# First mixer: products for the block inverse right behind the keys, and a planner that counts PSUM banks

## The chip, the cores and the metric

The kernel runs on one core of one Trainium2 chip. The metric is the device time of one execution in microseconds (us). The engines are named as the profile names them: PE is TensorE (matmuls; PEld its weight loads), DVE is VectorE, ACT is ScalarE, POOL is GpSimd, SP is SyncE, which here only issues DMA transfers. Each engine works through its own list of instructions in order; they wait for each other on semaphores.

## The reference

The reference is a decoder trunk of two layers on 1024 tokens of width 1024, each layer a mixer and a SwiGLU feed-forward, with a final norm. The change lies in the mixer of layer 0, where two groups of eight heads share one input projection and one output projection:

```python
z = h @ w_in
z_ret, z_rwkv = z[..., :4 * RET_WIDTH], z[..., 4 * RET_WIDTH:]
...
o = chunk_retention(q, k, heads(v))
ret_out = head_group_norm(o, RET_GN_EPS).reshape(B, T, RET_WIDTH) * jax.nn.silu(g)
...
y = rwkv7_scan(r_h, heads(decay), k_h, v_h, -kk, kk * heads(a))
y = head_group_norm(y, RWKV_GN_EPS, ln_g, ln_b)
bonus = jnp.sum(r_h * k_h * r_k, axis=-1, keepdims=True) * v_h
rwkv_out = (y + bonus).reshape(B, T, RWKV_WIDTH) * gate

return jnp.concatenate([ret_out, rwkv_out], axis=-1) @ w_out
```

The scan updates a 64x64 state per head at every token with a decay and a rank-one delta rule. The kernel computes it in chunks of 64 tokens: within a chunk the delta rule is a triangular system, whose matrix is the masked product of the scaled keys with each other, and this has to be inverted.

## The kernel before, in words

The 1024 tokens are worked on in two halves of 512 (`hf` 0 and 1). The hidden state is stored transposed, eight tiles of 128 channels by 512 tokens. The input projection of a half is 30 jobs, and a job is one tile `ps_f` of 128 columns by 512 tokens: eight contraction steps with three matmuls each (weights and inputs are split into a high and a low part), 24 matmuls. Both halves together make the 1440 matmuls `ps_f<-n,w` of line 218. The weights of half 0 are split once and parked in DRAM (`wsp`), and half 1 loads them back.

Behind the projection stand two kinds of chains, written as Python generators that yield between their steps:
- `pair` (once for each pair of RWKV heads, four in a half): the low-rank products `wua`, the norm of the keys (line 606), the scaled tiles AR and BK (lines 630 to 640), the bonus sum `bv` (lines 651 to 653), then GG, the products BK x AR of both halves of the chunk, masked by DVE (line 668), their diagonal 32x32 blocks copied to DRAM (`dn`, line 674), and transposes of BK, AR and v (XA and UV).
- `unit` (once for two pairs; units 0 and 1 are of half 0, units 2 and 3 of half 1): the blocks come back from `dn` with one matrix per partition (DT, line 747), DVE inverts them in 62 small operations X (lines 758, 762), they go out to `dg` and back into the tiles GT (lines 766, 773), and transposes and two rounds of small products, TZ,GG and GT,TZ (`ps_c`), fill in the off-diagonal block. Then follow the products of XA, UV and GG with GT, the recurrence over the eight chunks (lines 852 to 859), y, its norm (lines 875 to 888) and the gate (lines 893 to 896), which is stored to `cat`.
- `ret` (once for each pair of retention heads) is a shorter chain of the same kind, from line 940 to 1024.
- `second_norm` squares and sums the inputs of half 1, takes their mean with one matmul over all channels (line 509 feeds it), loads the inputs again (line 521) and writes the normed high and low parts (lines 433, 434).

The order of the work is set when the program is built, by the class `Plan`. It keeps a made-up clock, `now`. It first offers a step to any generator whose needs have been met (named events with a delay behind each) and whose own yield delay has passed; if none is due, it emits three matmuls of the current projection job. The delays are numbers in the code, in us. What is emitted is the order on every engine, and on SP's queue; at run time the engines wait for each other wherever the plan was wrong. PSUM's eight banks are four for the small products (`ps_m`), three for `ps_f` and one for `ps_c`, each kind used in turn: the fifth `ps_m` waits until the first has been read.

When the projection jobs are through, the output projection of half 0 (lines 319 to 321, 24 matmuls for each of eight tiles) fills PE beside the last unit, and that of half 1 follows. From the output projection of half 1 on, the rest of the program (feed-forward, attention layer, second feed-forward) is emitted in an order of its own.

Of the kernel before, what the change touches and what calls it, by code (L numbers as in the profile page):

```python
# [104 lines left out]
class Plan:  # L105
# [3 lines left out]
    def __init__(self, K):  # L109
        self.K, self.now, self.ev = K, 0.0, {}  # L110
        self.gens, self.jobs, self.cur, self.ahead = [], deque(), None, 0
# [53 lines left out]
    def run(self):  # L165
        while self.gens or self.jobs or self.cur:
            nxt = []
            for g in self.gens:
                t = self.time(g[1], g[2])
                if t is not None and t <= self.now:  # L170
# [6 lines left out]
                if t is not None:  # L177
                    nxt.append(t)
# [8 lines left out]
class Kern:  # L187
    def __init__(self, ctx, tc, A, out):
# [12 lines left out]
        self.h = [None, None]  # L201
# [67 lines left out]
    def pst(self, tag, shape):  # L269
        return self.t(self.ps, shape, "ps_" + tag, self.psb[tag])  # L270
# [227 lines left out]
    def second_norm(self):  # L498
        nc = self.nc
        yield (("y0", 0.0),), 0.0  # L500
        acc = self.t(self.pp, [P, HT], "nq", 4)
        for k in range(KT):
# [7 lines left out]
            yield (), 3.0  # L510
        ps = self.pst("m", [P, HT])
# [39 lines left out]
    def shifted(self, hf, ti, nm, p):  # L551
# [25 lines left out]
        self.plan.job(f"{nm}{hf}_{p}", hf, 16 + ti, lambda: self.nT, evac, ((f"n{hf}", 0.0),))  # L577
# [5 lines left out]
    def pair(self, u, hf, p):  # L583
# [31 lines left out]
        yield (), 6.0  # L615
# [25 lines left out]
        yield ((f"r{hf}_{p}", 5.0), (f"v{hf}_{p}", 5.0)), 8.0  # L641
# [4 lines left out]
        yield (), 12.0  # L646
        if u:
            yield ((f"y{u - 1}", 1.0),), 0.0
# [5 lines left out]
        S.copy(vp[:, 0:64], vp[:, HT : HT + 64])  # L654

# [14 lines left out]
        dn = self.dns[u]  # L670
        for e in range(2):
            for b in range(2):
                q, r0 = (p % 2) * 4 + e * 2 + b, 64 * e + 32 * b
                nc.sync.dma_start(
                    dn[q * 8 : q * 8 + 8].rearrange("c s t -> s c t"), GG[r0 : r0 + 32, :, e, 32 * b : 32 * b + 32]
                )
        self.plan.done(f"n{u}_{p}")
# [47 lines left out]
        yield (), 5.0  # L725
# [9 lines left out]
    def unit(self, u, hf, pairs):  # L735
# [7 lines left out]
        yield tuple((f"n{u}_{p}", 3.5) for p in pairs), 0.0  # L743
# [4 lines left out]
        X = self.t(mp, [P, 16, 32], "X", 2)  # L748
# [6 lines left out]
        for j in range(31):  # L755
# [7 lines left out]
            if j % 2:  # L763
                yield (), 2.4
        for q in range(2):
            nc.sync.dma_start(dg.rearrange("u (i q) t -> q u i t", q=2)[q], X[64 * q : 64 * q + 64])
        GTs = [self.t(mp, [P, NCH, 64], "GT", 2) for _ in pairs]
# [8 lines left out]
        yield tuple((f"a{u}_{p}", 1.0) for p in pairs), 7.0  # L776
# [3 lines left out]
        for GT in GTs:  # L780
            TZ = self.t(mp, [P, 2, NCH, 32], "X", 2)
# [920 lines left out]
```

## Time and profile before

| | us |
|---|---|
| median of 3 runs | 2527.07 (2525.83 to 2533.37) |
| the profiled execution | 2525.36 |
| its span, first to last instruction | 2523.6 |
| PE busy | 2352.1 (93%) |
| DVE, ACT, POOL busy | 1629.1, 1037.1, 1315.3 |
| first mixer, from the start to the norm behind it | 0 to 788 |
| PE busy in the first mixer | 704.6 |

The profiled execution is 1.7 us under the median, and 1.8 us of it lie outside the span. A number of the profile counts each f32 matmul as two instructions, so a group that the program writes as 16 matmuls of 64x64 stands there as x32; the projection's matmuls, whose inputs are split already, count once. The granted clock (PEclk) is the share of full speed at which PE was let run: in a stretch of 0.5 a matmul takes twice its time.

### The profile page before, as it was taken

The numbers are of one execution on the slowest core, as the hardware profiler recorded it, in microseconds if no ns is written. First come the engines' busy times: TensorE is split into PE (matmuls) and PEld (weight loads), VectorE is DVE, ScalarE is ACT, GpSimd is POOL, SyncE is SP. The second block draws the span as 40 slices with busy tenths as digits, with TensorE's granted clock in tenths as the row PEclk, the third lists the DMA queues.
The fourth block names the chain that finished last, engine by engine and source line by source line (L and its number), as shares of the span: only waits on it lengthen the run. The fifth ranks groups of instructions, "written<-read, shape, count | busy, mean of one in ns | idle before, by whom it ended". The sixth has DMA issues, their size and how long they took to land.

```text
span 2523.6 us, 35280 instructions
## 1 busy us (share of the span) xinstructions
PE 2352.1 (93%) x12850; PEld 1833.2 (73%) x12850; DVE 1629.1 (65%) x2387; ACT 1037.1 (41%) x1907; POOL 1315.3 (52%) x1048
## 2 busy tenths in 40 slices
PE   8888798999888999999999999899998999998996
PEld 6666565776666778887778776677686788886785
DVE  3666855756446337878685448547627788777776
ACT  5344433233454433333333545446635233333335
POOL 6554331221446656776576433242247577767664
PEclk9999998999999999999999999999999999999998
DMA  7564552533344545564474222131235456646652
GB/s 279 184 202 145 162 182 86 152 133 104 122 161 152 200 150 179 200 217 155 151 270 167 94 76 68 42 131 68 98 133 172 144 200 216 218 176 220 247 205 86
DMA packets 169035, 400.61 MB, mean 159 GB/s; under 512 B 43040, under 2 KB 45728, under 8 KB 168864
## 3 DMA queue, kind: packets, MB, share of 16 engines
q1 hardware_dynamic: 165744, 392.87, 45.0%
q10 hardware_dynamic: 2832, 4.45, 0.5%
q8 instruction: 102, 1.67, 0.3%
q0 software_dynamic: 288, 1.05, 0.1%
q14 instruction: 69, 0.57, 0.1%
HBM read 272.34 MB, written 120.59 MB: 156 GB/s over the span
## 4 chain that ended last, share of the span: by engine, by line
PE 69%; DVE 14%; DMA 5%; ACT 5%; issue 3%; POOL 3%; SPq 1%; DVEq 0%; ACTq 0%; POOLq 0%
PE ps_f L218 6%; PE ps_m L1085 6%; PE ps_m L1086 6%; PE ps_m L1087 6%; PE ps_f L319 5%; PE ps_m L218 5%; PE ps_f L320 5%; PE ps_f L321 5%; PE ps_f L1086 3%; PE ps_f L1085 3%; PE ps_f L1087 3%; PE ps_r L1085 2%; PE ps_r L1086 2%; PE ps_r L1087 2%; PE ps_c L1085 2%
## 5 line engine op out<-in xcount | busy, mean ns | idle before, releaser
L305 POOL TENSOR_TENSOR w<-wr,w 128x512 fp32r<-128x512 f32 (+1 forms) x276 | 369.7, 1346 | 495.5 <-ACT w L304 456.1
L218 PE MATMUL ps_f<-n,w 128*128 128x512 f32 x1440 | 378.9, 412 | 5.2 <-DMA w<-wsp 3.9
L218 PEld LDWEIGHTS ps_f<-n,w 128*128 128x128 f32 x1440 | 268.6, 192 | 82.4 <-issue 19.6
L304 ACT CAST w<-wr 128x512 fp32r<-128x512 f32 (+1 forms) x276 | 166.6, 611 | 260.5 <-PE ps_f L321 147.9
L319 PE MATMUL ps_f<-n,w 128*128 128x512 f32 x496 | 199.9, 407 | 8.8 <-ACT n L325 4.3
L320 PE MATMUL ps_f<-n,w 128*128 128x512 f32 x496 | 198.7, 401 | 0.0
L1085 PE MATMUL ps_f<-n,w 128*128 128x512 f32 x453 | 181.5, 403 | 17.9 <-ACT u L1234 13.0
L321 PE MATMUL ps_f<-n,w 128*128 128x512 f32 x496 | 197.1, 399 | 0.3 <-POOL w L305 0.3
L1086 PE MATMUL ps_f<-n,w 128*128 128x512 f32 x453 | 179.7, 397 | 9.0 <-DVE n L327 6.3
L1087 PE MATMUL ps_f<-n,w 128*128 128x512 f32 x453 | 179.8, 398 | 5.9 <-POOL w L305 5.9
L305 POOL TENSOR_TENSOR w<-wq,w 128x512 fp32r<-128x512 f32 x86 | 124.1, 1455 | 37.2 <-ACT w L304 20.8
L1092 DVE TENSOR_TENSOR nq<-ps_m,u 128x512 f32<-128x512 f32 x88 | 58.7, 684 | 113.3 <-PE ps_m L1087 113.3
L327 POOL TENSOR_TENSOR n<-nq,n 128x512 fp32r<-128x512 f32 x69 | 115.3, 1683 | 16.5 <-ACT n L325 16.5
L1085 PEld LDWEIGHTS ps_f<-n,w 128*128 128x128 f32 x453 | 86.0, 190 | 46.6 <-ACT u L1234 18.4
L319 PEld LDWEIGHTS ps_f<-n,w 128*128 128x128 f32 x496 | 95.1, 192 | 33.9 <-ACT n L325 4.7
L320 PEld LDWEIGHTS ps_f<-n,w 128*128 128x128 f32 x496 | 95.0, 192 | 24.4 <-issue 4.7
L321 PEld LDWEIGHTS ps_f<-n,w 128*128 128x128 f32 x496 | 94.6, 191 | 23.0 <-issue 1.9
L1086 PEld LDWEIGHTS ps_f<-n,w 128*128 128x128 f32 x453 | 86.2, 190 | 29.2 <-DVE n L327 6.7
L1087 PEld LDWEIGHTS ps_f<-n,w 128*128 128x128 f32 x453 | 86.1, 190 | 26.9 <-POOL w L305 7.6
L1085 PE MATMUL ps_m<-cb,w 128*128 128x512 f32 x232 | 93.3, 402 | 9.5 <-DVE nq L1092 9.5
L1246 POOL TENSOR_TENSOR w<-wd,w 128x512 fp32r<-128x512 f32 (+1 forms) x53 | 75.4, 1429 | 47.3 <-ACT w L1245 43.5
L1087 PE MATMUL ps_m<-cb,w 128*128 128x512 f32 x232 | 93.1, 401 | 0.0
(503 smaller groups left out, 6136.3 us busy)
## 6 DMA issues: line engine op xcount, KB each, us to landing
hc<-n SPq DMA_DIRECT2D x74, 512.0 KB, 2.6
wsp<-w SPq DMA_DIRECT2D x60, 512.0 KB, 3.2
w<-wsp SPq DMA_DIRECT2D x60, 512.0 KB, 3.4
wq<-in_w_gate SPq DMA_DIRECT2D x44, 512.0 KB, 4.4
u<-u SPq DMA_DIRECT2D x88, 256.0 KB, 2.8
n<-hc SPq DMA_DIRECT2D x43, 512.0 KB, 5.7
hid<-n SPq DMA_DIRECT2D x66, 256.0 KB, 2.0
ha<-hc SPq DMA_DIRECT2D x33, 512.0 KB, 6.6
```

The lines of the kernel that those rows point to most:

```text
L218: i = self.nc.tensor.matmul(out, lhsT, rhs, **kw)
L304: nc.scalar.copy(hi[:, :n], raw[:, c])
L305: nc.gpsimd.tensor_tensor(out=lo[:, :n], in0=raw[:, c], in1=hi.bitcast(F32)[:, :n], op=ALU.subtract)
L319: nc.tensor.matmul(ps, hi, rh, start=k == 0, stop=False)
L320: nc.tensor.matmul(ps, hi, rl, start=False, stop=False)
L321: nc.tensor.matmul(ps, lo, rh, start=False, stop=k == n - 1)
L327: e.tensor_tensor(out=lo, in0=src, in1=hi.bitcast(F32), op=ALU.subtract)
L1085: mm(ps, hi, xh, start=first and k == 0, stop=False, skip_group_check=True)
L1086: mm(ps, hi, xl, start=False, stop=False, skip_group_check=True)
L1087: mm(ps, lo, xh, start=False, stop=last and k == len(w) - 1, skip_group_check=True)
L1092: add = lambda o, x, y: V.tensor_tensor(out=o, in0=x, in1=y, op=ALU.add)
L1246: nc.gpsimd.tensor_tensor(out=lo, in0=v, in1=hi.bitcast(F32), op=ALU.subtract)
```

## The change

It has five parts.

1. **Products of their own for the blocks** (`nd`). Right behind BK, each pair computes its key-by-key products into one PSUM tile (16 matmuls of 64x64), DVE masks them (line 665 after the change), and the diagonal blocks go to `dn` from there, in four transfers. Before, they were cut out of GG, which comes after r and v have been projected, after `bv`, and in a later unit after the unit before it has ended (`y` of that unit). GG is computed as before; the tile `nd` comes from the pool `rt`, of six buffers.
2. **Banks counted.** Each step that takes a `ps_m` tile notes it as taken for 3 us of the made-up clock. A generator is stepped only while fewer than three are taken, unless no projection work is ready.
3. **Other delays.** Most yields are longer: behind the keys 8 to 12, before the keys' norm 6 to 8.5, `retk` 9 to 14, `retq` 9 to 12, TZ,GG to GT,TZ 2.5 to 6.5, the recurrence's step 1.3 to 2.0, the norm of y 3 to 6. Those of the inversion are shorter, 2.4 to 1.9.
4. **The inversion's places.** X gets one buffer, and TZ a tile of its own of half the size. GT's part waits until the unit before has written y.
5. **The second half.** Its norm may start when the last v of half 0 is projected instead of with y of unit 0, with 9 us before its matmul, and its jobs are due 4 us after the norm instead of at once.

The core of the diff:

```diff
+    def room(self):
+        self.banks = [t for t in self.banks if t > self.now]
+        return len(self.banks) < 3
...
+    def busy(self):
+        if self.cur is not None:
+            return self.cur["k"] < len(self.cur["rhs"])
+        if not self.jobs:
+            return False
+        t = self.time(self.jobs[0]["need"], 0.0)
+        return t is not None and t <= self.now
...
-                if t is not None and t <= self.now:
+                if t is not None and t <= self.now and (self.room() or not self.busy()):
...
     def pst(self, tag, shape):
+        if tag == "m" and self.plan:
+            self.plan.banks.append(self.plan.now + 3.0)
...
     def second_norm(self):
-        yield (("y0", 0.0),), 0.0
+        yield (("v0_3", 0.0),), 0.0
...
+        yield (), 9.0
         ps = self.pst("m", [P, HT])
         self.mm(ps, self.cst["ones"], acc, start=True, stop=True)
...
         G.tensor_tensor(out=s, in0=cs, in1=s, op=ALU.subtract)
-        yield (), 6.0
+        yield (), 8.5
...
         V.tensor_tensor(out=BK[:, :, 1, :], in0=c3(k), in1=c3(cs), op=ALU.mult)
-        yield ((f"r{hf}_{p}", 5.0), (f"v{hf}_{p}", 5.0)), 8.0
+        yield (), 12.0
+
+        ps = self.pst("m", [P, NCH, 64])
+        for c in range(NCH):
+            for rs in half:
+                self.mm(ps[rs, c, :], BK[rs, c, 0, :], AR[rs, c, 0:64], start=True, stop=True)
+        nd = self.t(mp, [P, NCH, 64], "rt", 6)
+        V.tensor_tensor(
+            out=nd, in0=ps, in1=self.cst["gmask"][:, 0:64].rearrange("p (o t) -> p o t", o=1).to_broadcast([P, NCH, 64]),
+            op=ALU.mult,
+        )
+        dn = self.dns[u]
+        for q in range(4):
+            r0 = 32 * q
+            nc.sync.dma_start(
+                dn[((p % 2) * 4 + q) * 8 : ((p % 2) * 4 + q) * 8 + 8].rearrange("c s t -> s c t"),
+                nd[r0 : r0 + 32, :, 32 * (q % 2) : 32 * (q % 2) + 32],
+            )
+        self.plan.done(f"n{u}_{p}")
+        yield ((f"r{hf}_{p}", 5.0), (f"v{hf}_{p}", 5.0)), 0.0
...
-        yield (), 12.0
+        yield (), 6.0
         if u:
-            yield ((f"y{u - 1}", 1.0),), 0.0
+            yield ((f"y{u - 1}", 2.0),), 0.0
...
         S.copy(vp[:, 0:64], vp[:, HT : HT + 64])
+        yield (), 2.5
...
-        dn = self.dns[u]
-        for e in range(2):
-            for b in range(2):
-                q, r0 = (p % 2) * 4 + e * 2 + b, 64 * e + 32 * b
-                nc.sync.dma_start(
-                    dn[q * 8 : q * 8 + 8].rearrange("c s t -> s c t"), GG[r0 : r0 + 32, :, e, 32 * b : 32 * b + 32]
-                )
-        self.plan.done(f"n{u}_{p}")
...
-        X = self.t(mp, [P, 16, 32], "X", 2)
+        X = self.t(mp, [P, 16, 32], "X", 1)
...
             if j % 2:
-                yield (), 2.4
+                yield (), 1.9
...
+        if u:
+            yield ((f"y{u - 1}", 0.0),), 3.0
         GTs = [self.t(mp, [P, NCH, 64], "GT", 2) for _ in pairs]
...
-            TZ = self.t(mp, [P, 2, NCH, 32], "X", 2)
+            TZ = self.t(mp, [P, NCH, 32], "TZ", 2)
...
-        yield (), 2.5
+        yield (), 6.5
         ps = self.pst("c", [P, 2, NCH, 32])
...
-            yield (), 1.3
+            yield (), 2.0
...
         self.plan.done(f"y{u}")
-        yield (), 3.0
+        yield (), 6.0
...
-        yield ((f"retk{hf}_{p}", 9.0), (f"retv{hf}_{p}", 6.0)), 0.0
+        yield ((f"retk{hf}_{p}", 14.0), (f"retv{hf}_{p}", 6.0)), 0.0
...
-        yield ((f"retq{hf}_{p}", 9.0),), 4.0
+        yield ((f"retq{hf}_{p}", 12.0),), 4.0
```

Line numbers move by 14 to 31. Three places show what the planner makes of it.

PE at the first pair of unit 0. Before, the bonus sum `ps_m` from `rr` is followed by GG's products of AR and BK with no other work between:

```order
L218 MATMUL ps_f_661<-n_33_150,w_614 128x512
L218 MATMUL ps_f_661<-n_29_146,w_614 128x512
L218 MATMUL ps_m_696<-rr_341,c_blk_129 128x512
L218 MATMUL ps_m_702<-AR_516,BK_520 128x128
L218 MATMUL ps_m_703<-AR_516,BK_520 128x128
```

After, the products nd (64x64) come ahead of it, and GG comes later. First the rows around nd:

```order
L232 MATMUL ps_f_622<-n_34_151,w_558 128x512
L232 MATMUL ps_f_622<-n_30_147,w_558 128x512
L232 MATMUL ps_m_641<-AR_528,BK_532 64x64 x16
L232 MATMUL ps_f_622<-n_31_148,w_558 128x512
L232 MATMUL ps_f_622<-n_35_152,w_558 128x512
```

and then those from the bonus sum on:

```order
L232 MATMUL ps_m_725<-rr_341,c_blk_129 128x512
L232 MATMUL ps_f_684<-n_31_148,w_616 128x512
L232 MATMUL ps_f_684<-n_35_152,w_616 128x512
L232 MATMUL ps_f_684<-n_31_148,w_616 128x512 x2
L232 MATMUL ps_f_684<-n_35_152,w_616 128x512
L232 MATMUL ps_f_684<-n_31_148,w_616 128x512
L232 MATMUL ps_f_756<-n_28_145,w_674 128x512
L232 MATMUL ps_f_756<-n_32_149,w_674 128x512
L232 MATMUL ps_f_756<-n_28_145,w_674 128x512 x2
L232 MATMUL ps_f_756<-n_32_149,w_674 128x512
L232 MATMUL ps_f_756<-n_28_145,w_674 128x512
L232 MATMUL ps_m_764<-AR_528,BK_532 128x128
```

Between the bonus sum and GG stand 12 projection matmuls now, and none before.

SP's queue at the change to half 1, around the end of unit 1's inversion (`dg<-X`). Before (`nq<-in_xT` of line 521 are the inputs of half 1, `r` retention's rotated tiles, `wsp` and `w` weights):

```order
L521 DMA nq_2899<-in_xT 128x512
L912 DMA r_438_2763<-r_437_2761 32x512 x4
L307 DMA wsp<-w_2775 128x1024
L521 DMA nq_2903<-in_xT 128x512
L521 DMA nq_2907<-in_xT 128x512
L766 DMA dg_162<-X_2529 1024x1x32 x2
L521 DMA nq_2911<-in_xT 128x512
L279 DMA wr_6398<-in_w_out 128x1024
L287 DMA w_2827<-wsp 128x1024
L773 DMA GT_3064<-dg_162 32x8x32 x2
```

After, where the inputs are line 538 and `dg` line 795:

```order
L303 DMA w_2907<-wsp 128x1024
L795 DMA dg_162<-X_2551 1024x1x32 x2
L1055 DMA cat_80<-r_440_2775 128x512
L303 DMA w_2909<-wsp 128x1024
L538 DMA nq_2957<-in_xT 128x512
L943 DMA r_453_2895<-r_452_2893 32x512 x4
L538 DMA nq_2961<-in_xT 128x512
L538 DMA nq_2965<-in_xT 128x512
L538 DMA nq_2969<-in_xT 128x512
L303 DMA w_3025<-wsp 128x1024
```

Three of the eight loads of inputs stood ahead of `dg<-X`, and now none does; a load of weights for half 1, `w<-wsp`, does. On DVE the eight operations that norm these inputs (line 434, after 450) stand behind the last operation of the inversion in both orders.

PE at the end of unit 3. Before (`ps_c` is the recurrence, `ps_m` from GG and AR the output y, `c_blk` the sum for its norm, `ps_f_6610` the last tile of half 0's output projection, `ps_f_6777` the first of half 1's):

```order
L321 MATMUL ps_f_6610<-n_936_6323,w_6607 128x512
L218 MATMUL ps_c_6204<-GT_5906,XA_5334 64x64 x2
L218 MATMUL ps_c_6204<-GT_5907,XA_5441 64x64 x2
L218 MATMUL ps_c_6211<-GT_5906,XA_5334 64x64 x2
L218 MATMUL ps_c_6211<-GT_5907,XA_5441 64x64 x2
L218 MATMUL ps_m_6218<-GG_5247,UV_5353 64x64 x16
L218 MATMUL ps_m_6219<-AR_4451,GT_5906 64x64 x16
L218 MATMUL ps_m_6257<-GG_5315,UV_5460 64x64 x16
L218 MATMUL ps_m_6258<-AR_4626,GT_5907 64x64 x16
L218 MATMUL ps_m_6296<-rt_6255,c_blk_129 128x512
L342 MATMUL ps_f_6673<-nq_6650,c_ones_67 128x512
L319 MATMUL ps_f_6777<-n_1010_6725,w_6771 128x512
```

After, with the norm's second sum, the gate's two products (`gup`) and what follows them:

```order
L336 MATMUL ps_f_6694<-n_955_6478,w_6691 128x512
L232 MATMUL ps_m_6451<-rt_6446,c_blk_129 128x512
L232 MATMUL ps_m_6456<-gl_3170,gup_143 128x512
L232 MATMUL ps_m_6462<-gl_3170,gup_143 128x512
L337 MATMUL ps_f_6694<-n_951_6474,w_6691 128x512
L335 MATMUL ps_f_6694<-n_952_6475,w_6691 128x512
L336 MATMUL ps_f_6694<-n_956_6479,w_6691 128x512
L337 MATMUL ps_f_6694<-n_952_6475,w_6691 128x512
L335 MATMUL ps_f_6694<-n_952_6475,w_6691 128x512
L336 MATMUL ps_f_6694<-n_956_6479,w_6691 128x512
L337 MATMUL ps_f_6694<-n_952_6475,w_6691 128x512
L335 MATMUL ps_f_6728<-n_949_6472,w_6722 128x512
```

Before, the output projection of half 0 had ended when unit 3's y was computed. After, 55 of its matmuls stand behind the gate's products, and 22 more between the two sums of the norm; only then comes half 1's.

More of the change, by code (lines that the diff above doesn't have):

```diff
@@ L109, in __init__ @@
     def __init__(self, K):
-        self.K, self.now, self.ev = K, 0.0, {}
+        self.K, self.now, self.ev, self.banks = K, 0.0, {}, []
         self.gens, self.jobs, self.cur, self.ahead = [], deque(), None, 0
@@ L775, in unit @@
             )
-        yield tuple((f"a{u}_{p}", 1.0) for p in pairs), 7.0
+        yield tuple((f"a{u}_{p}", 0.0) for p in pairs), 6.0
         sts = [self.st[hf, p] for p in pairs]
```

24 lines of the change are left out of this document (12 added, 12 removed).

## The prediction

> **What bounds the kernel now.** I read the page first: engines, then the chain that ended last.
>
> ```profile
> span 2523.6 us, 35280 instructions
> PE 2352.1 (93%) x12850; PEld 1833.2 (73%) x12850; DVE 1629.1 (65%) x2387; ACT 1037.1 (41%) x1907; POOL 1315.3 (52%) x1048
> PE 69%; DVE 14%; DMA 5%; ACT 5%; issue 3%; POOL 3%; SPq 1%; DVEq 0%; ACTq 0%; POOLq 0%
> ```
>
> PE is busy 93% of the span and leads the chain, so the time is PE's work, plus its idle time, plus what it works at half clock. Behind the first mixer the orders of all engines are the same before and after, so everything is decided up to 788 us. The table by stages gives, for each stretch of the mixer, its length, PE's busy time and the granted clock:
>
> ```profile
> core 0: us, PE busy (x), PEclk, DMA share, GB/s
> 0.00:160.00 160.00, 139.85 (x799) 0.95 0.66 227
> 160.00:240.00 80.00, 71.15 (x614) 0.96 0.47 163
> 240.00:280.00 40.00, 35.38 (x446) 0.96 0.41 126
> 280.00:340.00 60.00, 46.18 (x255) 0.89 0.74 236
> 340.00:390.00 50.00, 49.24 (x503) 1.00 0.34 117
> 390.00:460.00 70.00, 59.74 (x504) 0.90 0.30 95
> 460.00:573.00 113.00, 109.36 (x1002) 1.00 0.43 136
> 573.00:637.00 64.00, 57.94 (x444) 0.95 0.39 115
> 637.00:788.00 151.00, 135.72 (x1017) 0.94 0.43 147
> ```
>
> Length less busy is idle: 20.2, 8.9, 4.6, 13.8, 0.8, 10.3, 3.6, 6.1 and 15.3, together 83.4, of which 6.6 us are the first wait for the norm. That 6.6 stays, so 76.8 us can change. The clock's term is at most length x (1 - PEclk): 8.0, 3.2, 1.6, 6.6, 0, 7.0, 0, 3.2, 9.1, together 38.7. Part of the slow time is idle and loses nothing; I take three quarters, 29 us. What the plan can win back is thus 76.8 + 29 = 106 us. The waits name the causes:
>
> ```profile
> PE ps_c L218 <- ACT X L796: 10.8, 3, 5.6
> PE ps_m L229 <- issue: 7.9, 2, 5.1
> PE ps_m L218 <- POOL nq L509: 7.2, 1, 7.2
> PE ps_m L218 <- DVE bv L653: 6.1, 3, 4.5
> PE ps_m L229 <- ACT rt L886: 5.6, 2, 2.8
> PE ps_m L218 <- ACT rt L886: 5.0, 4, 3.5
> PE ps_f L319 <- ACT n L325: 4.3, 1, 4.3
> PE ps_m L218 <- DMA GT<-dg: 3.2, 1, 3.2
> PE ps_m L218 <- ACT rt L606: 2.5, 1, 2.5
> ```
>
> All are small products emitted before their inputs were ready, with projection matmuls queued behind them that could have run. A delay put right gets such a wait back whole, as long as work is left to put ahead.
>
> **The clock.** PE's own list shows what a wait costs beyond itself:
>
> ```profile
> 74.07 1.12 PE L218 MATMUL ps_m<-rt,c_blk 128*128 128x512 f32 x2 [2.47 <-ACT rt L606]
> 74.64 2.64 PE L218 MATMUL ps_f<-n,w 128*128 128x512 f32 x9
> 85.06 2.07 PE L218 MATMUL ps_m<-AR,BK 64*128 64x128 f32 x14 [4.53 <-DVE bv L653]
> 192.63 1.92 PE L218 MATMUL ps_c<-GT,X 32*32 32x32 f32 x64 [5.59 <-ACT X L796]
> 194.48 5.04 PE L218 MATMUL ps_f<-n,w 128*128 128x512 f32 x12
> 273.46 0.95 PE L218 MATMUL ps_f<-n,w 128*128 128x512 f32 x3
> 274.34 1.15 PE L218 MATMUL ps_m<-UV,GG 64*64 64x64 f32 x32
> 275.42 1.66 PE L218 MATMUL ps_f<-n,w 128*128 128x512 f32 x6
> 277.00 1.09 PE L218 MATMUL ps_m<-r,r 128*64 128x128 f32 x16
> ```
>
> Behind the idle 5.59 us, 12 projection matmuls took 5.04 us, 0.42 each; behind 2.47 us, nine took 2.64, 0.29 each. From 275.42 to 277.00 six take 1.58 us and from 273.46 to 274.34 three take 0.88, so one is 0.23 and each group costs some 0.18 beside. I price each wait of about 3 us or more with 1.7 to 3.4 us of lost clock, as the 12 matmuls show (12 x 0.19 = 2.3), and shorter ones with none.
>
> **Part by part: what is added on PE.** nd is eight products of 16 matmuls. The row at 274.34 is the same form, 64x64, 32 counted, and takes 1.08 us to the next: 8 x 1.08 = 8.6 us. The finer weave cuts the projection into 149 groups instead of 121 up to its end: 28 x 0.2 = 5.6 us. Sum +14.2 us; nothing hides it, since PE is the bound.
>
> **What is added elsewhere.** DVE masks nd, eight times the form of line 668, and the dn transfers are the same number from another tile:
>
> ```profile
> sum 788.00, PE 704.56 PEld 530.55 DVE 468.04 ACT 321.15 POOL 304.20; mean PE 78.28 PEld 58.95 DVE 52.00 ACT 35.68 POOL 33.80
> L668 DVE TENSOR_TENSOR GG<-ps_m,c_gmask 128x512 f32<-128x512 f32 x32 | 20.6, 683 | 3.4 <-PE ps_m L218 3.4
> L674 SPq DMA_DIRECT2D dn<-GG x32: 303/421/648, 90.6 to 594.1; - x32
> ```
>
> DVE gets 8 x 0.68 = 5.5 us more, between waits (it is idle 320 of the 788 us), so I cost it at nothing on the path; without that cover it would be at most 5.5. SP issues the same 32 transfers of 0.42, earlier in its queue. They hold the `rt` buffer until they land; the next pair's keys wait for it only if six are in use, between 0 and the 2 us of a landing; I take 0. Smaller X and TZ tiles move no work: 0. TZ's own buffer lets TZ be written without waiting for X; whatever it brings is in the stages.
>
> **What is moved, stage by stage.** For each stretch I went through the new order on PE, DVE, ACT and SP, set each product against the engine that feeds it with durations of this trace, and asked what would still wait. "Before" is idle plus clock from the table (a quarter off its bound), "after" an estimate of that working.
>
> - 0 to 160: 13.6 + 6 = 19.6. The waits of 5.11 (retention's transposes, now due 14 us behind the keys), 2.47 and 4.53 are covered: 12 projection matmuls (2.8 us) now stand between the bonus sum and GG. Left are GG's last bank behind `bv`, since `bv` still stands behind an operation that waits for ACT (2.5), the transposes of BK (2.3) and AR (1.7), starts (1.6), and clock 1.7: 9.8.
> - 160 to 240: 8.9 + 2.4 = 11.3. The 5.59 goes: between TZ,GG and GT,TZ the new order has 7.3 us of other work (retention's products and projection) where 12 projection matmuls, 2.8 us, stood. The recurrence's steps keep about half: 3.6.
> - 240 to 280: 4.6 + 1.2 = 5.8. The two norms of y still load ACT tables in turn (Ln, Exp); two of the gate's products now wait for the second, and the transposes behind them for a bank: 6.6.
> - 280 to 340, the change to half 1: 13.8 + 5 = 18.8. The 7.24 for the norm's sum goes, since the sum over the inputs is started earlier and given 9 us more. But SP's loads of half 1's inputs now all stand behind `dg<-X`, which waits for the last operation of unit 1's inversion:
>
> ```profile
> 305.23 2.07 PE L218 MATMUL ps_m<-nq,c_ones 128*128 128x512 f32 x2 [7.24 <-POOL nq L509]
> L766 SPq DMA_DIRECT2D dg<-X x2: 582/622/663, 310.8 to 311.5; - x2
> L434 DVE SCALAR_TENSOR_TENSOR n<-nq,pv,n x8: 721/744/753, 313.1 to 330.1; 128x512 fp32r<-128x512 f32 x8
> ```
>
> Already before, the eight norming operations came 2.3 to 19.3 us behind the inversion; they pace the first job of half 1. Now the first comes some 5 us behind, and PE arrives about 4 us after the inversion ends (44 us of matmuls and their breaks against some 48 of transfers and inversion). A job of 24 x 0.23 = 5.5 us then stretches to about 16: 12 to 14 lost, 2 of clock, 2 of others, less what its neighbours fill: 18. Bounds are 6 (the loads pass the inversion's end quickly) and 30.
> - 340 to 390: 0.8; after 1.5.
> - 390 to 460, unit 1's end: 10.3 + 5.3 = 15.6. The gate's banks wait for DVE behind the second norm's Exp: 13.
> - 460 to 573: 3.6; after 5, GT,TZ and one weight load.
> - 573 to 637, unit 2's end: 6.1 + 2.4 = 8.5; two operations of retention are ahead of the norm on ACT: 10.3.
> - 637 to 788: 15.3 + 6.8 = 22.1.
>
> ```profile
> 670.92 1.92 PE L218 MATMUL ps_c<-GT,X 32*32 32x32 f32 x64 [4.32 <-ACT X L796]
> 741.66 1.22 PE L319 MATMUL ps_f<-n,w 128*128 128x512 f32 x2 [4.27 <-ACT n L325]
> ```
>
> Unit 3's inversion starts earlier, so its chain meets half 0's output projection sooner: 55 matmuls (about 12 us) stand behind the gate and cover its way through `cat` into `n`; the 4.27 and its clock go, and 30 matmuls (6.9 us) stand where nothing covered the 4.32. Four steps of the recurrence stand back to back (3 to 4 us), some clock: 7.
>
> Before: 19.6 + 11.3 + 5.8 + 18.8 + 0.8 + 15.6 + 3.6 + 8.5 + 22.1 = 106. After: 9.8 + 3.6 + 6.6 + 18 + 1.5 + 13 + 5 + 10.3 + 7 = 75. Won 31, paid 14: 17 us. The profiled execution's 2525.4 becomes 2508; the median lies 1.7 above it, so **2510 us**. What can be told from no change here is 0.3%, 7.6 us.
>
> **Rivals.**
> 1. The delays hold at face value: most waits go, as the plan's numbers say. Then of 106 some 40 stay (start, the half change, table loads): -66 + 14 = -52, **2475 us**. For it: the ends at 85, 192, 305, 670 and 741 each are waits shorter than the delay now added. Against: at the unit ends the new order puts the same readers behind ACT's table loads, and unit 1's end has the same two late products. Chance 0.15.
> 2. The waits only move: DVE, with inversion, GG and bonus sums now more closely interleaved in one queue, delays as many products as before; 106 becomes 92, which pays for nd and the breaks: **2527 us**. Chance 0.12.
> 3. Slower, by one mechanism: the change to half 1. Since neither loads nor norming can pass unit 1's inversion, PE stands idle until it ends plus up to 19 us, while GG, bonus sums and transposes of both pairs now stand among its operations on DVE and wait for PE. It decides from 25 us more than my 18, 43 us in that stretch, which is an inversion ending some 25 us later than I have it: **2540 us**. For it: the queue rows; against it: nd starts the inversion earlier in PE's work. Chance 0.14.
> 4. The finer weave keeps PE at a lower clock. The stretch 340 to 390 is woven as finely (503 matmuls) and was granted 1.00, against it. At half clock in 40 more us, +20: **2530 us**. Chance 0.03. [...]
>
> **How the numbers follow.** The forecast has 0.56: 2510, its own range 2494 to 2524 (the stages' 31 won between 47 and 17). Range for 8 in 10: 2478, which leaves out the better half of rival 1, to 2538, which leaves out the upper half of rival 3. Faster by over 0.3% (under 2519.5): 0.85 of the forecast, 0.48, rival 1 with 0.15, and 0.02 of rival 2: 0.65. Within: 0.17, the forecast's upper end (0.05), most of rival 2 (0.07), 0.02 of rival 4 and 0.03 of rival 3. Slower (over 2534.7): 0.18, the rest of rivals 3, 2 and 4 (0.15) and a tail of the forecast.
>
> **What would show it.** Right: PE idle up to the norm behind the mixer falls by some 20 us, with no wait for `bv` of over 3 us, none of over 2 for ACT's TZ copy, none for the norm's sum, none at the output projection of half 1; 256 more counted 64x64 matmuls, near 8.6 us; and one stretch of 15 to 20 us idle or slow where half 1 begins, whose releaser is the norming of the inputs. Wrong: nd's matmuls or the breaks over 20 us; a wait of unit 1 or 2 for a bank that grew beyond 6 us; a DVE that is never idle during the inversions.

## The result and the profile after

The changed kernel takes 2533.34 us (median of 15 runs, 2525.74 to 2540.38), the kernel before 2527.07 us in 15 runs of the same job; the ratio is 1.0016, with a 95% interval from 1.0003 to 1.0028. That is within the 0.3% called no change, on the slower side of it. The forecast was 2510 us. The profiled execution has a span of 2531.5 us, 7.9 more than before. The norm's matmul behind the mixer starts at 797.6 us instead of 788.0, so the mixer is 9.6 us longer, and the rest 1.7 shorter.

Two rows of the table by stretches, each from the start to that norm, first before, then after (columns: length, PE busy, granted clock, DMA share, GB/s):

```profile
0.00:788.00 788.00, 704.56 (x5565) 0.95 0.48 160
```

```profile
0.00:797.60 797.60, 718.96 (x5821) 0.94 0.48 158
```

PE is busy 14.4 us longer and idle 78.6 instead of 83.4 us. So the growth of the busy time is near the 14.2 foreseen (what it is made of comes below), and of the waits, 4.8 us have gone. Behind the first wait for the norm, which stayed (6.5 us), the waits of the changed kernel carry other names:

```profile
PE ps_m L232 <- DVE GG L705: 8.0, 4, 2.8
PE ps_m L243 <- DVE GG L705: 6.3, 3, 3.1
PE ps_m L232 <- DVE bv L689: 6.0, 2, 5.9
PE ps_f L232 <- DVE n L450: 5.0, 3, 2.4
PE ps_m L232 <- DVE UV L852: 4.9, 4, 2.2
PE ps_f L335 <- ACT n L341: 4.8, 2, 4.2
PE ps_c L232 <- DVE X L791: 4.2, 1, 4.2
```

Of the nine causes listed for the kernel before, the copies of TZ, the norm's sum, and retention's transposes are gone from the top. What stands there now are products that wait until DVE has emptied a bank (GG), the inputs of the next stage (n), and a step of the recurrence (`ps_c`, released behind an operation X of the inversion). The table by stages, to be read against the prediction's:

```profile
0.00:165.00 165.00, 144.24 (x867) 0.94 0.65 218
165.00:240.00 75.00, 70.59 (x762) 1.00 0.52 182
240.00:290.00 50.00, 40.74 (x308) 0.87 0.47 154
290.00:340.00 50.00, 40.80 (x299) 0.90 0.71 218
340.00:400.00 60.00, 60.00 (x581) 1.00 0.38 123
400.00:465.00 65.00, 56.37 (x490) 0.87 0.33 100
465.00:580.00 115.00, 107.89 (x1050) 0.99 0.44 128
580.00:640.00 60.00, 57.25 (x513) 0.94 0.39 118
640.00:797.60 157.60, 141.08 (x975) 0.92 0.40 140
```

### The profile page after: what moved, and what is told of

It is laid out like the page before. It is cut to its first block, busy times and chain, and to the rows that moved or that the text cites. A ratio compares the mean times of both kernels' runs of the same rounds, so it can differ in the third digit from the quotient of the medians.

```text
span 2531.5 us, 35775 instructions
## 1 busy us (share of the span) xinstructions
PE 2366.0 (93%) x13106; PEld 1841.1 (73%) x13106; DVE 1624.5 (64%) x2395; ACT 1038.2 (41%) x1907; POOL 1317.1 (52%) x1048
## 4 chain that ended last, share of the span: by engine, by line
PE 69%; DVE 14%; DMA 6%; ACT 5%; issue 3%; POOL 2%; SPq 1%; DVEq 0%; ACTq 0%; POOLq 0%
PE ps_f L232 7%; PE ps_m L1116 6%; PE ps_m L1117 6%; PE ps_m L1118 6%; PE ps_f L336 5%; PE ps_f L335 5%; PE ps_f L337 5%; PE ps_m L232 4%; PE ps_f L1117 3%; PE ps_f L1116 3%; PE ps_f L1118 3%; PE ps_r L1116 2%; PE ps_r L1117 2%; PE ps_r L1118 2%; PE ps_c L1118 2%
## 5 line engine op out<-in xcount | busy, mean ns | idle before, releaser
L232 PE MATMUL ps_f<-n,w 128*128 128x512 f32 x1440 | 395.5, 421 | 10.5 <-DVE n L450 5.0
L335 PE MATMUL ps_f<-n,w 128*128 128x512 f32 x496 | 199.8, 406 | 11.4 <-ACT n L341 4.8
L336 PE MATMUL ps_f<-n,w 128*128 128x512 f32 x496 | 201.0, 406 | 1.6 <-POOL n L343 1.4
L337 PE MATMUL ps_f<-n,w 128*128 128x512 f32 x496 | 199.2, 403 | 0.3 <-POOL w L321 0.3
L1116 PE MATMUL ps_f<-n,w 128*128 128x512 f32 x453 | 182.0, 404 | 16.8 <-ACT u L1265 11.8
L1117 PE MATMUL ps_f<-n,w 128*128 128x512 f32 x453 | 180.1, 398 | 8.6 <-DVE n L343 5.8
L1118 PE MATMUL ps_f<-n,w 128*128 128x512 f32 x453 | 180.0, 399 | 5.9 <-POOL w L321 5.9
L337 PEld LDWEIGHTS ps_f<-n,w 128*128 128x128 f32 x496 | 95.6, 193 | 22.9 <-issue 2.3
```

The costliest lines, as they stand in the source:

```text
L232: i = self.nc.tensor.matmul(out, lhsT, rhs, **kw)
L335: nc.tensor.matmul(ps, hi, rh, start=k == 0, stop=False)
L336: nc.tensor.matmul(ps, hi, rl, start=False, stop=False)
L337: nc.tensor.matmul(ps, lo, rh, start=False, stop=k == n - 1)
L1116: mm(ps, hi, xh, start=first and k == 0, stop=False, skip_group_check=True)
L1117: mm(ps, hi, xl, start=False, stop=False, skip_group_check=True)
```

## The experiments

The theories. **A**: the new order trades one wait for another of about the same price, and nd costs PE its own work. **B**: nd's earlier inversion is what gains, and the delays lose it. **C**: the counting of banks holds the idle time down. **D**: the wait at the mixer's end is a mistake of order that can be put right. **E**: the delays gain much, which nd and the counting lose. **F**, for the last four runs: PE's idle total stays the same whatever is done. Every kernel was timed against the kernel before on the same chip, in five sessions in which the kernel before had medians of 2527.1 to 2529.2 us; the ratio is to that, with its interval. Two rows of the table that differ by some 2 us are not told apart.

| kernel | median us | ratio |
|---|---|---|
| the change | 2533.3 | 1.0016 (1.0003 to 1.0028) |
| before + nd | 2558.2 | 1.0120 (1.0101 to 1.0139) |
| before + nd, delay 12 | 2549.2 | 1.0074 (1.0059 to 1.0089) |
| the change without nd | 2526.1 | 0.9991 (0.9979 to 1.0002) |
| the change without counting | 2529.5 | 1.0004 (0.9992 to 1.0017) |
| delays alone | 2527.4 | 0.9992 (0.9979 to 1.0004) |
| the change, nd's matmuls twice | 2542.5 | 1.0042 (1.0026 to 1.0059) |
| the change, bonus sum later | 2531.4 | 1.0015 (1.0003 to 1.0026) |
| the change, gate later | 2535.1 | 1.0026 (1.0017 to 1.0035) |
| the change, second norm as before | 2534.3 | 1.0028 (1.0016 to 1.0040) |
| the change, output projections joined | 2532.5 | 1.0025 (1.0012 to 1.0038) |
| before, output projections joined | 2552.0 | 1.0103 (1.0087 to 1.0118) |
| without nd, output projections joined | 2547.0 | 1.0079 (1.0064 to 1.0095) |
| before, one exponential | 2512.7 | 0.9935 (0.9923 to 0.9948) |
| the change, one exponential | 2532.3 | 1.0015 (1.0005 to 1.0024) |
| delays alone, one exponential | 2523.6 | 0.9984 (0.9971 to 0.9996) |
| without nd, one exponential | 2527.4 | 0.9991 (0.9981 to 1.0001) |

### The parts of the change, alone and taken out

First nd alone, put into the kernel before at BK, with the delay of 8 that stood there; `dn` is written from it, and no longer from GG.

```diff
-        yield ((f"r{hf}_{p}", 5.0), (f"v{hf}_{p}", 5.0)), 8.0
+        yield (), 8.0
+        (nd's products, mask and dn transfers as in the change)
+        yield ((f"r{hf}_{p}", 5.0), (f"v{hf}_{p}", 5.0)), 0.0
```

> The kernel before with one part of the change alone: the products nd behind the keys, and the dn transfers from them; planner, delays and tiles as before. Theory A (the waits only move, and nd costs PE its own work): 8 x 1.08 = 8.6 us of matmuls and up to 3 of breaks, little back, since before the inversion's end was waited for at one place only (4.3 us at unit 3's TZ,GG): 2531 to 2538. Theory B (the earlier inversion is what gains, and the delays lose it): under 2522.

Measured: 2558.2 us, 30 more than before and worse than either theory said. The longest waits of that kernel:

```profile
PE ps_m L218 <- DVE BK L634: 18.2, 6, 6.1
PE ps_m L218 <- DVE bv L672: 10.6, 4, 5.1
PE ps_f L319 <- DVE h L548: 10.5, 1, 10.5
```

nd waits for BK, which DVE has not finished 8 us of the plan after the keys, and the mixer's end has a wait of 10.5 us for half 0's result (`h`). So one delay of the change was given to it, 12 for 8:

> The kernel before with nd alone (measured 2558), and with one delay of the change beside it: 12 instead of 8 between BK and nd. In the trace of nd alone PE waits for BK's product on DVE at 66, 202, 258, 423, 522 and 545 us (6.1, 2.4, 2.5, 2.2, 3.9, 1.1: 18.2 us) and runs 24 us at half clock behind them. If these waits are why nd alone costs 30 us and not its 8.8, the time falls by 20 to 28: 2530 to 2538. If other products wait in their place, it stays above 2548.

Measured: 2549.2 us, 9 less, not 20 to 28. The wait for BK is off the top of the list; in its place stands the bonus sum, and the wait for `h` is still there (12.6 us):

```profile
PE ps_m L218 <- DVE bv L672: 29.3, 6, 11.4
```

That is theory A in one step. Next the other way about: the change without nd, the change without the counting of banks (the edit below), and the change without both, which leaves the delays:

```diff
-                if t is not None and t <= self.now and (self.room() or not self.busy()):
+                if t is not None and t <= self.now:
```

> The changed kernel without nd: the dn transfers come from GG again, all delays and the counting of banks stay. Theory A: 9 to 14 us off the changed kernel, 2519 to 2524. Theory B: the chains start later and wait, 2538 or more. Idle time of PE in the mixer within 10 us of the changed kernel's 79 by A, above 90 by B.

> The changed kernel with the condition on free banks taken out, so that a generator is stepped as soon as its delay has passed. Theory A (one wait is traded for another): 2530 to 2537, the waits at other products. Theory C (the counting keeps products from waiting for banks, and is what holds the idle time down): 2543 or more, with more waits whose releaser is a DVE or ACT evacuation of GG, XA or UV.

> The changed kernel without nd and without the counting of banks: the new delays and tiles alone. Theory A (the delays trade waits, nd costs its own work): 2522 to 2530, no different from before. Theory E (the delays gain some 25 us that nd and the counting lose again): 2505 to 2515.

Measured: 2526.1, 2529.5 and 2527.4 us. Without nd the new order is as fast as the old one, with or without counting (theory A had up to 2524 for the first, 2 us less); with nd, the counting brings nothing (2533.3 with, 2529.5 without). B, C and E fall. In the profile of the change without nd (first), and of the delays alone, PE's row up to the norm is

```profile
0.00:789.00 789.00, 708.69 (x5564) 0.95 0.50 160
```

```profile
0.00:786.40 786.40, 708.34 (x5565) 0.95 0.49 160
```

so idle are 80.3 and 78.1 us instead of 83.4, and busy some 4 more than before's 704.6 with the same matmuls: what the order wins in waits it pays in busy time, by a lower clock or by breaks between groups, which these rows do not separate. nd then adds 10.3 us of busy time (718.96 against 708.69). Its price was also measured by issuing its matmuls a second time into the same tile:

> The changed kernel with nd's matmuls issued twice into the same tile, everything else the same: 8 x 16 more matmuls of 64x64. If nd costs PE its own time and nothing hides it, 8.6 to 9 us more than the changed kernel: 2540 to 2544. If nd falls into waits that PE has anyway, under 4 us more.

Measured: 2542.5 us, 9.1 more than the change (6.6 by the two ratios). So nothing of note hides nd. The groups agree (the same view of the change and of the doubled one: matmuls, busy us, mean ns):

```profile
L232 PE MATMUL ps_m<-AR,BK 64*64 64x64 f32 x256 | 9.5, 226 | 2.1 <-DVE BK L651 2.1
```

```profile
L232 PE MATMUL ps_m<-AR,BK 64*64 64x64 f32 x512 | 18.3, 231 | 3.9 <-DVE BK L651 3.9
```

The sum is less clean than the group. In the profiled execution the doubled kernel's mixer is 8.5 us longer (806.1 us), of which only 4.5 are busy time (723.45) and 4.0 are idle: the other groups ran a little faster, and other waits grew.

### Three waits of the new order, put right one by one

Behind its start, the longest wait of the change is at 92 us, in the first unit, on PE and on DVE:

```profile
92.39 2.07 PE L232 MATMUL ps_m<-AR,BK 64*128 64x128 f32 x14 [5.88 <-DVE bv L689]
```

```profile
91.04 0.69 DVE L645 TENSOR_TENSOR rt<-rt,rt 128x512 f32<-128x512 f32 x1 [10.42 <-ACT rt L638]
```

DVE stands 10.4 us at the next pair's keys, which wait for two table loads of 1.28 us, a logarithm and an exponential on ACT (87.15 to 91.01 us); the bonus product `bv` behind it, whose sum PE finished at 81.4 us, started at 91.65. The 12 projection matmuls that stand between the bonus sum and GG cover part of that only. ACT itself is late because of nd. Its operation ahead of that logarithm writes a tile of the pool `rt`, and had to wait until nd, which holds the buffer, had been read by the `dn` transfers:

```profile
85.33 0.63 ACT L640 ACTIVATE rt<-rt 128x512 f32<-128x512 f32 x1 [4.17 <-DMA dn<-rt]
```

DVE had masked nd by 79.4 us. SP issued the four transfers from 81.8 us on, behind a transfer of weights that waited for POOL, and the last landed at 85.2. In the change without nd the same DVE operation, there at 85.67 us, stands half as long, and PE has no wait for `bv` there:

```profile
85.67 0.69 DVE L645 TENSOR_TENSOR rt<-rt,rt 128x512 f32<-128x512 f32 x1 [5.46 <-ACT rt L638]
```

So an estimated 4.2 of the 5.88 us are the price of nd's buffer, which the prediction had at 0, and 1.7 are left of the kind that it priced at 2.5. A second wait comes from nd in another way. At 553 us a step of unit 2's recurrence stands on DVE behind unit 3's inversion, which is due earlier with nd and whose first operation holds DVE until the blocks are back from `dn`:

```profile
549.88 0.19 DVE L787 TENSOR_TENSOR xt<-X,DT 128x31 f32<-128x31 f32 x1 [5.91 <-DMA DT<-dn]
553.17 0.69 PE L232 MATMUL ps_c<-GT,XA 64*64 64x64 f32 x8 [4.21 <-DVE X L791]
```

The experiment that follows moves the bonus sum only, and leaves the buffer as it is. With the bonus sum planned behind the keys:

```diff
-        yield (), 6.0
+        yield (), 12.0
         if u:
```

> The changed kernel with one delay put back: 12 instead of 6 between the scaling of r and the bonus sum, so that the bonus product on DVE stands behind the next pair's keys instead of between them and an operation that waits for ACT. If that wait is the cause of the 5.88 us at 92 us and of the 17.1 us at half clock that begin there, it falls under 2 us, the half clock there under 7 us, and the mixer is 8 to 12 us shorter: 2522 to 2526, if nothing else moves. By theory A another product waits in its place and the time stays within 4 us of the changed kernel's 2533.

Measured: 2531.4 us, 2 less than the change, within its noise. The wait for `bv` at this place is replaced by two others:

```profile
95.44 1.38 PE L232 MATMUL ps_m<-AR,BK 64*64 64x64 f32 x32 [3.97 <-DVE BK L651]
102.31 0.48 PE L232 MATMUL ps_m<-AR,BK 64*128 64x128 f32 x2 [2.63 <-DVE bv L689]
```

nd of the next pair, which needs those same keys, now waits in front; ACT waits 4.18 us for `dn` as before. No run gave nd a buffer of its own, so what that alone would win is not shown. Two more waits were treated like this one. First the gate's products, delayed:

```diff
             S.activation(q, q, AF.Exp, scale=-0.5)
-        yield (), 0.5
+        yield (), 5.0
```

> The changed kernel with 5 instead of 0.5 between the norm of y and the gate's products, once a unit. At unit 0's end PE waits 3.66 us for the bank that the second logarithm on ACT reads, and 2.02 behind it, with 10.2 us at half clock. If that is a wait to be planned away, it goes, with its like at units 1 and 2, for 5 to 10 us: 2523 to 2528. By theory A the time stays within 4 us of 2533.

Measured: 2535.1 us; nothing won. At unit 0's end the waits of 3.66 and 2.02 us are gone, and the transposes of BK wait 4.42 for the same logarithm on ACT. And the second norm, back at its old place and without its delays:

> The changed kernel with the second half's norm as before: it starts with y of unit 0, has no 9 us ahead of its matmul, and half 1's jobs are due at once. If the early start is what shortened the change to half 1 (idle 13.8 us before, 9.2 after), the wait for the norm's sum of 7.2 us returns and the time rises by 5 to 10: 2538 to 2543. If the norm's place does not matter there, because the loads of inputs behind the inversion pace it, it stays at 2530 to 2536.

Measured: 2534.3 us, so by its expectation the norm's place does not matter. The trace says that it does, and that the rest makes up for it. The wait for the norm's sum returns:

```profile
313.32 2.07 PE L232 MATMUL ps_m<-nq,c_ones 128*128 128x512 f32 x2 [6.30 <-POOL nq L525]
```

In the stretch around the change to half 1, first of the change and then with the norm at its old place, PE gets 5.5 us less done, at a lower clock:

```profile
280.00:350.00 70.00, 58.50 (x458) 0.90 0.59 184
280.00:350.00 70.00, 53.00 (x351) 0.85 0.59 183
```

Unit 1's TZ,GG starts at 354.2 instead of 344.5 us. Behind it the kernel with the old place runs at a clock of 0.97 instead of 0.94, and the two mixers end within 1.4 us of each other. So the early norm shortened its own stage, and that came to nothing at the end: again theory A. The old place also lets the wait at 252 us fall from 3.66 to 2.30: in the change, ACT has the squaring of its inputs ahead of the exponential of unit 0's end and waits there for a transfer,

```profile
247.76 0.64 ACT L524 ACTIVATE nq<-nq 128x512 f32<-128x512 f32 x1 [2.45 <-DMA nq<-in_xT]
```

which I had not looked for when I costed the earlier norm.

### The mixer's end

The forecast's greatest gain was here. The changed kernel does compute unit 3 earlier, and the 4.3 us for TZ's copy are gone. But the waits at this place are no shorter. PE waits 10.6 us in all between 730 and 753 us, where it waited 4.27 and 0.78 at 742 before:

```profile
732.37 1.13 PE L358 MATMUL ps_f<-nq,c_ones 128*128 128x512 f32 x2 [2.65 <-DVE nq L356]
737.66 1.22 PE L335 MATMUL ps_f<-n,w 128*128 128x512 f32 x2 [4.17 <-ACT n L341]
```

```profile
733.53 0.69 ACT L359 ACTIVATE rs<-ps_f,c_eps 128x512 f32<-128x512 f32 x1 [1.13 <-PE ps_f L358]
736.99 0.62 ACT L341 CAST n<-nq 128x512 fp32r<-128x512 f32 x1 [0.83 <-DMA nq<-cat]
```

The casts that half 1's output projection needs stand on ACT behind the norm of half 0's result (lines 359 and 360, with two table loads), which needs half 0's last tile; the first of them then waits 0.83 us more for its load from `cat`. The 55 matmuls that were to cover the way from the gate through `cat` are that half's own projection: when they end, the norm follows, and only then the casts. With half 1's projection emitted ahead of that norm, so that the two output projections are joined:

```diff
-        K.form0("n2a", K.factor_of(0, sp, "f"), K.n8(K.pp), sp)
         K.h[1] = K.wout(1, K.n8(nb), K.s8(hy, "h1", 2))
+        K.form0("n2a", K.factor_of(0, sp, "f"), K.n8(K.pp), sp)
```

> The changed kernel with two statements exchanged: the output projection of half 1 is emitted ahead of the norm and the scaled inputs of half 0. Theory D: at the mixer's end of the changed kernel PE waits at 732 to 752 us (2.65 for the norm's sum, 4.17 and about 3.8 more for casts and weights) and runs at half clock for 17 us, because the casts of half 1's inputs stand behind the norm's logarithm on ACT. With them ahead of it these waits go: 8 to 14 us less than the changed kernel, 2519 to 2525, and the idle time there under 3 us. Theory A (one wait is traded for another): the norm of half 0 then comes late, the feed-forward waits for it behind the projection, and the time stays within 4 us of 2533.

> The kernel before with the same exchange of two statements. Its wait at the mixer's end is 4.27 + 0.78 + 0.75 us and half clock for 6.8 us. Theory D: 5 to 8 us less than before, 2519 to 2522. Theory A: within 4 us of 2527.

> The changed kernel without nd (measured 2526) and with the exchange of the two statements. Its last projection waited 7.1 (for h), 7.0 (for the norm's rs) and 1.5 us. Theory D: the 7.0 and its half clock go, 8 to 11 us: 2515 to 2518. Theory A: within 4 us of 2526.

Measured: 2532.5, 2552.0 and 2547.0 us. In the change, the gap closes and opens again behind: two stretches, of the change and then of the exchange,

```profile
690.00:770.00 80.00, 68.88 (x369) 0.85 0.45 163
770.00:860.00 90.00, 79.16 (x328) 0.98 0.45 156
```

```profile
690.00:770.00 80.00, 79.17 (x460) 0.97 0.43 149
770.00:860.00 90.00, 70.39 (x254) 0.87 0.49 171
```

10.3 us more busy up to 770 us and 8.8 less behind it, where the feed-forward waits for the same norm. D falls: it is a step of one chain, and whatever stands ahead of it only moves the wait. In the other two orders the exchange loses 20 to 24 us, which neither D nor A foresaw. Much of it lies between 700 and 900 us: with the exchange the kernel before is idle 28.7 us there instead of 17.7, at a clock of 0.93 and 0.90 in the two halves instead of 0.97 and 0.98, and the projection of half 1 waits 6.8 us for its first casts (8.9 in the order without nd). Why the casts come later still in these two orders is open.

### Taking latency out of the chain

All these waits are for steps of chains that pass between PE, ACT and DVE. The last four runs leave the order and shorten one step. At a unit's end ACT computes a logarithm and an exponential for each of two pairs, in turn, with four table loads of 1.28 us. The program emits both logarithms before both exponentials; ACT ran them alternately, as at unit 1's end of the kernel before:

```profile
407.07 0.69 ACT L886 ACTIVATE rt<-ps_m,c_eps 128x512 f32<-128x512 f32 x1
409.07 0.63 ACT L888 ACTIVATE rt<-rt 128x512 f32<-128x512 f32 x1
411.01 0.69 ACT L886 ACTIVATE rt<-ps_m,c_eps 128x512 f32<-128x512 f32 x1
```

So the order that the plan emits is not the order on every engine, although the text ahead of the prediction says so. With both pairs' norms in one tile (the inversion's DT, free at that time), one exponential serves both and has to wait for both logarithms, and two loads are left:

```diff
+        q2 = self.t(mp, [P, 32, 32], "DT", 1).rearrange("p (u a) b -> p u (a b)", u=2)
...
-            q = self.t(mp, [P, HT], "rt", 6)
+            q = q2[:, len(ys), :]
...
-        for y, q in ys:
-            S.activation(q, q, AF.Exp, scale=-0.5)
+        S.activation(q2, q2, AF.Exp, scale=-0.5)
```

> The kernel before with the two norms of y in one tile (taken from the inversion's DT), so that one exponential serves both and ACT loads two tables at a unit's end instead of four: 2 x 1.28 us less on ACT, three units with PE waiting for it (2.8, 3.5, 2.8 us and half clock of 3.4 to 10.2 us behind them). Theory A (order only trades waits, since all of them are steps of one chain): taking latency out of the chain itself does not trade, and 4 to 10 us are won, 2518 to 2523. Theory F (PE's idle total stays near 80 us whatever is done): within 4 us of 2527.

> The changed kernel with the same single exponential. At unit 0's end it waits 3.66 and 2.02 us with 10.2 us at half clock, at units 1 and 2 2.6 to 3.1 us. Theory A: 4 to 10 us less than the changed kernel, 2523 to 2529. Theory F: within 4 us of 2533.

> The new delays and tiles without nd and without the counting of banks (measured 2527), with the single exponential: theory A 2517 to 2523, under both kernels; theory F 2523 to 2531.

> The new delays and the counting of banks without nd (measured 2526), with the single exponential: theory A 2516 to 2522, under both kernels; theory F 2522 to 2530.

Measured: 2512.7, 2532.3, 2523.6 and 2527.4 us. On the kernel before it wins 0.65%, more than foreseen, and that kernel beats both; on the three new orders 1.0 and 3.8 us less and 1.3 more, within the runs' noise. Neither A nor F holds for all four: F's ranges miss the kernel before; A's miss all four, that one on the better side. The edit also takes two tiles from the pool `rt`, which no run separates from the loads. Loads on ACT for the logarithms (those for the exponentials fall alike, from 8 to 4), before and with one exponential:

```profile
L886 ACT ACT_TABLE_LOAD x8 | 10.3, 1283 | 8.3 <-PE ps_m L218 8.2
```

```profile
L887 ACT ACT_TABLE_LOAD x4 | 5.1, 1283 | 4.3 <-PE ps_m L218 4.3
```

Unit 1's end, 400 to 440 us, in the kernel before and with one exponential:

```profile
400.00:440.00 40.00, 31.45 (x187) 0.83 0.19 63
```

```profile
400.00:440.00 40.00, 36.95 (x259) 1.00 0.40 122
```

There PE waited for the banks that the two logarithms read (1.26 and 3.45 us, and then 10.2 us at half clock), and the second logarithm stood behind the first exponential and two loads. With one exponential it follows the first at once; these waits are gone, and in this stretch 5.5 us of idle time and the lost clock are back. Over the mixer, PE's idle time falls from 83.4 to 74.2 us. In the change, the gate's own wait at unit 0's end fell from 3.66 to 0.17 us, and the transposes of BK behind it, which need a bank that DVE empties, waited 4.82 instead of 2.02:

```profile
249.80 1.12 PE L232 MATMUL ps_m<-gl,gup 128*128 128x512 f32 x2 [0.17 <-ACT DT L918]
255.75 1.71 PE L243 MATMUL ps_m<-c_ident,BK 64*128 64x64 f32 x16 [4.82 <-DVE GG L705]
```

So in the new order a DVE step has become the late one at this place. Why the old order lets the gain through and the new ones do not, these runs do not settle.

## Why the prediction was wrong

- **What bounds the kernel**: right. The rest of the program moved by 1.7 us only.
- **nd on PE, 8.6 us**: right; 9.5 us in its rows, 9.1 by doubling.
- **nd elsewhere, taken at 0: wrong.** The prediction said that the next pair's keys wait for nd's buffer only if six are in use, 0 to 2 us, and took 0. ACT waited 4.17 us for it at 85 us, and PE's longest wait follows from that; the inversion that nd brings forward held DVE for 5.91 us at 550 and PE for 4.21. No wait of PE bears the name of `dn`, so a list of PE's waits does not show either.
- **Breaks, 5.6 us**: with the clock, the busy time beside nd grew by some 4 to 5 us (708.7 against 704.6 without nd; 718.96 - 9.5 against 704.6 with it). The two cannot be told apart here. By the prediction's own rule the clock rows alone give 35 us after and 29 before, which is more than the growth; no run shows the 5.6 of the breaks.
- **The stages: wrong, and this is the step that failed.** "Won 31" was 4.8 of idle time and nothing of the clock. By the same rule (idle plus three quarters of what the clock row gives, without the start) the nine stages after are 21.7, 4.4, 14.2, 13, 0, 14.9, 8, 5.5 and 26, together 108; the prediction had 75, and 106 before. Three terms make the error. 0 to 165: 21.7 for 9.8, since PE still waits 5.88 us for `bv`, with half clock for 17.1 us around and behind it; I had priced that wait at 2.5 by the matmuls put ahead, without asking how long DVE stands (10.4 us) and what holds ACT ahead of it (nd's buffer, 4.17). Unit 0's end: 14.2 for 6.6; PE waits 3.66 us for the second logarithm's bank, since the squaring of half 1's inputs stands on ACT ahead of the first exponential (2.45 us for their load), and half clock for 10.2 us follows. The mixer's end: 26 for 7, since I covered the gate's way to `cat` and did not ask what else stands ahead of the casts on ACT; that ACT has the norm of half 0 there could be read from the order.
- **The change to half 1**: 13 for 18, the mechanism right and the size 5 us too high: the norming paces half 1's first job (5.0 us in three waits, and 4.2 at the first cast). Rival 3 did not come.
- **Clock, none behind waits under about 3 us**: wrong, as the last section shows.
- **Rivals.** Rival 2 is what happened, with 0.12: the waits moved. It had 92 for their sum, where 108 came, and 2527, where 2533 came. Its reason, a DVE queue more closely woven, is half of it; ACT's queue is the other. Rival 4's 40 us more at half clock are the author's estimate, which no run shows: up to the norm PE had 95.6 us of half clock after and 78.5 before, 17.1 more, and no run tells whether the finer weave has a part in that. That 2533 lies within the range for 8 in 10 is owed to that range's width, which was drawn for rival 3, and not to the working.

## What to carry over

A wait that disappears from one row is won only if the next instruction of the same chain is ready too: cost a new order by following each feeding engine's own queue up to the instruction that PE waits for, and look at what that engine is itself waiting for, before counting matmuls put in between. A tile that is borrowed from a shared pool is such a wait: nd's buffer was free again only when its last reader, a DMA transfer, was done, and ACT stood 4.17 us for it. Take the parts of such a change apart first: here delays and counting were worth nothing, and the added products cost their full 9 us. Taking two table loads of 1.28 us each out of the way of a step that PE is seen waiting for won more than any reordering of the plan, but only in the order in which it was the late one.

## What the runs showed of the hardware

Half clock also came behind shorter waits than in the first mixer of the kernel before, where the shortest was 2.76 us (at 638.6); later in that trace it began at 1236.5 us in a wait of 1.27, with one of 1.57 ahead of it. In the change it began at 71.8 us behind an idle of 2.09, and at 419.9 behind 1.58 and 1.39:

```profile
71.23 1.54 PE L232 MATMUL ps_m<-AR,BK 64*64 64x64 f32 x32 [2.09 <-DVE BK L651]
419.57 1.74 PE L232 MATMUL ps_m<-rt,c_blk 128*128 128x512 f32 x2 [1.39 <-ACT rt L909]
```

```profile
71.80:75.20 3.40, 3.40 (x26) 0.50 0.17 71
88.90:106.00 17.10, 11.06 (x75) 0.50 0.39 139
419.90:423.30 3.40, 3.40 (x7) 0.51 0.00 0
```

In the clock records of the two profiles, PE has 12 stretches of half clock up to the norm before and 13 after, and each is 3.4, 6.8, 10.2 or 17.1 us long: 1, 2, 3 or 5 times 3.4. The longest began in the wait of 5.88 and lasted through two more of 0.64 and 1.91 with small groups between them. The length of a wait alone does not tell whether half clock follows: behind 2.47 us at 74.1 us in the kernel before, the granted clock stayed at 1.00 until 82.8, and behind 2.09 us in the change came 3.4 us of half clock. What decides it, these runs do not show. A matmul at half clock took somewhat less than twice its time, which the text ahead of the prediction gives it: in the kernel before, those in a row from 1237.5 to 1239.6 us stand 0.43 us apart, those from 1227.2 to 1232.1, at full clock, 0.23.

The second thing is the order itself. The output projection is emitted after the whole plan, and yet its matmuls stand on PE between unit 3's steps (in the kernel before from 643.9 us on, with unit 3's GT,TZ at 670.9); and ACT's logarithms and exponentials ran in another order than the program emits them (407.07, 409.07 and 411.01 us above). The plan's own matmuls are marked in the kernel to stay in program order, the output projection's matmuls and most of the other engines' work are not. So the framework schedules once more between the plan and the engines, and a delay in the plan reaches the engines' queues only in part.
